# Linear attention in a hybrid decoder trunk: the products of two levels, and those between token tiles, sent in one burst

## The chip, the cores and the metric

The kernel runs on one core of a Trainium2 chip, as one launch. The metric is the device time of one execution in microseconds, the median of several runs. Engines are named as in the profile: TensorE is PE (its weight loads PEld), VectorE DVE, ScalarE ACT, GpSimd POOL, SyncE SP.

## The reference

Two layers (DEPTH), 512 tokens, a width of 2048. Each layer normalises its input, multiplies it by one input projection, feeds three groups of heads from the result (a short convolution, a stick-breaking attention, a gated linear attention), gates each of them, and puts the concatenation through an output projection into the residual stream. The change lies in the gated linear attention, which has four heads with 64 key and 128 value columns:

```python
g = jax.nn.log_sigmoid((gl_lr @ gla_w_up + gla_b_up)) / GLA_TAU
def step(state, inp):                       # one chunk of 64 tokens
    qc, kc, vc, gc = inp
    cum = jnp.cumsum(gc, axis=2)
    o_inter = jnp.einsum("bhck,bhkv->bhcv", qc * jnp.exp(cum), state)
    diff = cum[:, :, :, None, :] - cum[:, :, None, :, :]
    decay = jnp.where(causal, jnp.exp(jnp.minimum(diff, 0.0)), 0.0)
    att = jnp.einsum("bhtk,bhsk,bhtsk->bhts", qc, kc, decay)
    o_intra = jnp.einsum("bhts,bhsv->bhtv", att, vc)
    ...
    return new_state, o_inter + o_intra
```

In words: each token attends to itself and all earlier ones, with a weight that is a product of query, key and a decay of its own for every key column. The output is normalised and gated before it joins the mix.

## The kernel before

**Projections.** The weights are in float32 and are streamed from memory, 256 columns at a time. ACT makes the high half of each block in float16 (`whi`, line 476, or `split` in `wsums`, line 530) and DVE the low half (`wlo`, line 483, or line 531). TensorE multiplies high by high, high by low and low by high, with the activations held as two halves too. These products use the whole array of 128 rows: lines 729 to 731 (`project_cols`), 740 to 742 (`tok_mm`), and line 822 or 825 (`prod` in `project_quick`, which uses seven products of half blocks where there were eight).

**The linear attention without a scan.** The weights of all pairs of tokens within a token tile of 128 are built by halving. At the level with half length `h` (64, 32, 16, 8, 4, 2, 1, in `LEV`) each block of 2h tokens splits into a source half and a target half; the decay between the two halves is the product of one factor of the source and one of the target, so that an ordinary product of matrices gives all weights of that level. DVE and ACT make both factors (the tile `e`; lines 1130 to 1139). Then each is split into two float16 pieces: the source by `split_src` (high on ACT, line 1095, low on DVE, line 1096; tile `qp` in the profile), the target by `split_tgt` (high on ACT, line 1101, low on DVE, line 1102; tile `th`). There are two slots for pieces, `src16[b]` and `tgt16[b]`, and the levels use them in turn, `b = li % 2`.

`mm3` (line 1104) does the products: three terms, each for the two heads of a pair. A head has 64 key columns, so each product of line 1109 uses 64 rows of the array and the two heads lie in different halves of it. A level needs four calls (one for each token tile) of six products, into a PSUM tile `aps` (`psz` in the profile, two buffers of two banks). A masked copy on DVE (line 1144) puts the level into `attd` (tile `zw`), which collects all levels. The diagonal (lines 1153 to 1163) follows; its products are on line 1158.

**Between token tiles** the weights factor with a single reference point, in two sets (`two` = 0 and 1, lines 1167 to 1179), with the same slots and the same `mm3`: four calls, lines 1186 to 1190. Their sums are read on ACT (line 1193) and DVE (line 1194); then line 1206 multiplies everything by the values.

All of this is done for two head pairs, `p` = 0 and 1, in each of the two layers. Work of other parts goes on at the same time.

**The order of the work.** Behind a short hand-ordered start a planner sets the order of each engine's queue, from an estimate of times and from priorities: work written earlier goes first if it is ready, and a block under `tc.high_priority` goes ahead of that. Every engine then takes its queue strictly in that order and waits where a semaphore isn't there yet. `order(a, b)` makes the planner place `a` behind `b`. In the kernel before, the products of `mm3` have no priority and no order of their own: the planner puts them in where they are ready, between products of the projection that is running at the time.

Of the kernel before, what the change touches and what calls it, by code (L numbers as in the profile page):

```python
# [11 lines left out]
ALU = mybir.AluOpType  # L12
# [5 lines left out]
P = 128  # L18
# [25 lines left out]
def hybrid_trunk(ctx, tc, x, norm_g, w_in, conv_w, conv_b, sb_qn_g, sb_kn_g,  # L44
                 gla_w_up, gla_b_up, gla_on_g, w_out, out):
    nc = tc.nc
    V, S, G, T = nc.vector, nc.scalar, nc.gpsimd, nc.tensor
# [3 lines left out]
    NT = seq // P  # L51
# [19 lines left out]
    def nm(s):  # L71
        uid[0] += 1
        return f"{s}_{uid[0]}"
# [4 lines left out]
    def wk(shape, tag, bufs=None, dt=F32):  # L78
        return work.tile(shape, dt, tag=tag, name=nm(tag), bufs=bufs)
# [7 lines left out]
    def bank2():  # L87
        return psz.tile([P, 2, 512], F32, tag="z", name=nm("psz"))
# [59 lines left out]
    HT = P // 2  # L148
# [132 lines left out]
    for h in range(2):  # L281
        mm = spread(h)
# [430 lines left out]
    for l in range(depth):  # L713
# [287 lines left out]
        for t, o, u in project_by_token(xh, xl, GX):  # L1001
# [16 lines left out]
        for p in range(2):  # L1018
# [3 lines left out]
            a = wk([P, seq], "ga")  # L1022
# [19 lines left out]
        src16 = [[scr[0][:, b, i, :] for i in range(2)] for b in range(2)]  # L1042
        tgt16 = [[scr[1][:, b, i, :seq // 2] for i in range(2)] for b in range(2)]
# [5 lines left out]
        for tag in ("qT", "kT"):  # L1049
            o = wk([P, 2, seq], tag)  # L1050
# [47 lines left out]
        def split_tgt(e, b):  # L1098

            hi, lo = tgt16[b]  # L1100
            S.activation(hi, e, AF.Copy)
            V.tensor_tensor(lo, e, hi, ALU.subtract)

        def mm3(o, sb, ss, tb, g0, g1):

            for i, (a, b) in enumerate(((0, 0), (0, 1), (1, 0))):
                for hh in range(2):
                    hs = slice(hh * HT, (hh + 1) * HT)
                    T.matmul(o[:, hh, :], src16[sb][a][hs, ss], tgt16[tb][b][hs, g0 * HT:g1 * HT], start=i == 0,
                             stop=i == 2, skip_group_check=True)  # L1110

        tsl = [slice(t * P, (t + 1) * P) for t in range(NT)]
        for p in range(2):
            Pp, q_, k_ = Pc[:, p, :], gq[:, p, :], gk[:, p, :]
            attd = wk([P, 2, NT, P], "zw")
            G.memset(attd, 0.0)

            for li, h in enumerate(LEV[:-1]):
                b = li % 2
                e = wk([P, 2, seq // 2], "e")  # L1120

                def sides(a):
                    a4 = a.rearrange("p (b s j) -> p b s j", s=2, j=h)
                    return a4[:, :, 0, :], a4[:, :, 1, :]

                (P0, P1), (k0, _), (_, q1) = sides(Pp), sides(k_), sides(q_)
                e0, e1 = (e[:, i, :].rearrange("p (b j) -> p b j", j=h) for i in range(2))
                if h > 1:
                    ref = P0[:, :, h - 1:h].to_broadcast([P, seq // (2 * h), h])
                    V.tensor_tensor(e0, P0, ref, ALU.subtract)  # L1130
                    V.tensor_tensor(e1, ref, P1, ALU.subtract)
                    S.activation(e, e, AF.Exp, scale=1.0 / TAU)
                    V.scalar_tensor_tensor(e0, e0, 1.0, k0, ALU.min, ALU.mult)
                    split_src(e0, lambda a: sides(a)[0], b)
                else:
                    V.tensor_tensor(e1, P0, P1, ALU.subtract)
                    S.activation(e[:, 1, :], e[:, 1, :], AF.Exp, scale=1.0 / TAU)
                    split_src(k_, lambda a: a, b)
                V.scalar_tensor_tensor(e1, e1, 1.0, q1, ALU.min, ALU.mult)
                split_tgt(e[:, 1, :], b)  # L1140
                aps = bank2()[:, :, :NT * HT]
                for t in range(NT):
                    mm3(aps[:, :, t * HT:(t + 1) * HT], b, tsl[t], b, t, t + 1)
                V.copy_predicated(
                    attd.rearrange("p h t (b s j) -> p h (t b) s j", s=2, j=h)[:, :, :, 1, :],
                    masks[:, li].rearrange("p (o t) (b j) -> p o (t b) j", o=1, j=h).to_broadcast(
                        [P, 2, NT * HT // h, h]),
                    aps.rearrange("p h (t b j) -> p h (t b) j", t=NT, j=h))

            e = wk([P, seq], "e")  # L1150
            V.tensor_tensor(e, q_, k_, ALU.mult)
            hi, lo = src16[1]
            S.activation(hi, e, AF.Copy, scale=2.0 ** -14)
            V.scalar_tensor_tensor(lo, e, 2.0 ** -14, hi, ALU.mult, ALU.subtract)
            aps = bank2()[:, 0, :2 * NT]
            for t in range(NT):
                for i, a in enumerate((hi, lo)):
                    T.matmul(aps[:, 2 * t:2 * t + 2], a[:, tsl[t]], heads, start=t == i == 0, stop=i == 1,
                             skip_group_check=True)
# [7 lines left out]
            for two, bias in ((0, (nT[:, p, 0:1], None, nT[:, p, 2:3], None)),  # L1167
                              (1, (nT01[:, p:p + 1], nT[:, p, 1:2], None, nT[:, p, 2:3]))):
                e = wk([P, 2, 256], "e")
                n = [0, 0]  # L1170
                for t in range(NT):
                    tgt = int(t >= 2 if two else t % 2)
                    et = e[:, tgt, n[tgt] * P:(n[tgt] + 1) * P]
                    n[tgt] += 1
                    S.activation(et, Pp[:, tsl[t]], AF.Exp, scale=(-1.0 if tgt else 1.0) / TAU,
                                 bias=bias[t] if bias[t] is not None else 0.0)
                    V.scalar_tensor_tensor(et, et, 1.0, (q_ if tgt else k_)[:, tsl[t]], ALU.min, ALU.mult)
                split_src(e[:, 0, :], lambda a: a[:, :256], two)
                split_tgt(e[:, 1, :], two)

            for i in range(NT):
                S.activation(att16[0][:, i], attd[:, :, i], AF.Copy, scale=2.0 ** -21)
                V.scalar_tensor_tensor(att16[1][:, i], attd[:, :, i], 2.0 ** -21, att16[0][:, i], ALU.mult, ALU.subtract)
            ax = [wk([P, 2, 512], tag, dt=F16) for tag in ("za", "za", "e")]
            aps = bank2()
            mm3(aps[:, :, :128], 0, tsl[0], 0, 0, 2)
            mm3(aps[:, :, 128:256], 0, tsl[1], 0, 2, 4)
            mm3(aps[:, :, 256:], 1, tsl[0], 1, 0, 4)
            aps2 = bank2()
            mm3(aps2[:, :, :256], 1, tsl[1], 1, 0, 4)  # L1190
            for a, o in zip(ax, (aps[:, :, :256], aps[:, :, 256:], aps2[:, :, :256])):
                hi, lo = (a[:, i].rearrange("p (h c) -> p h c", h=2) for i in range(2))
                S.activation(hi, o, AF.Copy, scale=2.0 ** -21)
# [2 lines left out]
            for hh in range(2):  # L1196
# [7 lines left out]
                for i, (cs, t, a) in enumerate(seqmm):  # L1204
                    for n, (vi, ai) in enumerate(((0, 0), (0, 1), (1, 0))):
                        T.matmul(ops_[:, cs], gv[p][:, vi, t, hh * P:(hh + 1) * P], a[ai], start=i == n == 0,
                                 stop=i == len(seqmm) - 1 and n == 2, skip_group_check=True)
# [181 lines left out]
        for j in range(4):  # L1389
# [21 lines left out]
            for n in range(2):  # L1411
# [11 lines left out]
                for b in range(2):  # L1423
# [149 lines left out]
```

## Time and profile before

| | us |
|---|---|
| median of 3 runs | 1629.07 (1628.01 to 1629.4) |
| the profiled execution | 1628.53 |
| its span, first to last instruction | 1626.7 |
| TensorE busy | 1614.1 (99%) |
| weight loads | 1355.0 (83%) |
| VectorE busy | 1446.8 (89%) |
| ScalarE busy | 1196.5 (74%) |
| GpSimd busy | 274.0 (17%) |

Busy times are of the profiled execution. A row of the timeline gives start and duration in us, the engine, the line, what is written and read, the shape, and how many instructions were merged in it; a bracket at its end tells how long the engine stood idle before it and what ended that. A TensorE instruction's duration spans its way through the array, and the next starts before it ends, so that distances between starts tell what a product costs. A table by stretch gives for each engine the busy time in it. The linear attention of layer 0 lies between 125 and 280 us of the span, that of layer 1 between 930 and 1090.

### The profile page before, as it was taken

Reading aid. Unit: us, or ns where it says so; the run is one execution under the profiler, and the core shown is the slowest. Engines: PE = TensorE matmul, PEld = TensorE weight load, DVE = VectorE, ACT = ScalarE, POOL = GpSimd, SP = SyncE. Lnnn points to the kernel's source line nnn. Section 1 sums busy time; section 2 is a strip of 40 time slices with the busy share of each in tenths; the row PEclk is TensorE's granted clock in tenths of the full one; section 3 lists DMA queues with packets and bytes.
Section 4 is the critical chain, followed back from the end, with each engine's and each line's share of the span. In section 5 each row is a group of like instructions: output and inputs, shape, how many; then the busy total and the mean of one; then the engine's idle time right before and its main releaser. Section 6 shows DMA issues by size and latency. Waiting matters only on the chain.

```text
span 1626.7 us, 42256 instructions
## 1 busy us (share of the span) xinstructions
PE 1614.1 (99%) x18205; PEld 1355.0 (83%) x18205; DVE 1446.8 (89%) x2411; ACT 1196.5 (74%) x1769; POOL 274.0 (17%) x305
## 2 busy tenths in 40 slices
PE   8999999999999999999999999999999999999998
PEld 6757768989898967799996668689898989668998
DVE  8989999989898979898699899898988889898896
ACT  8579887868787776666775788788787868676573
POOL 0122121121212122011102111211121211220110
PEclk9999999999999999999999999999999999999999
DMA  7335245476867677544734444545777786773441
GB/s 264 106 78 168 67 125 132 122 143 154 149 148 164 150 169 216 157 156 144 238 89 114 121 118 118 138 84 142 152 159 157 154 166 154 167 226 127 156 157 54
DMA packets 193643, 235.98 MB, mean 145 GB/s; under 512 B 90242, under 2 KB 153036, under 8 KB 192944
## 3 DMA queue, kind: packets, MB, share of 16 engines
q0 software_dynamic: 79904, 181.42, 42.1%
q1 hardware_dynamic: 104544, 42.42, 13.0%
q10 hardware_dynamic: 9008, 9.45, 1.7%
q8 instruction: 142, 2.33, 0.6%
q14 instruction: 45, 0.37, 0.1%
HBM read 179.65 MB, written 14.68 MB: 119 GB/s over the span
## 4 chain that ended last, share of the span: by engine, by line
PE 79%; DVE 11%; ACT 6%; issue 2%; DMA 1%; POOL 0%; SPq 0%; DVEq 0%; ACTq 0%; POOLq 0%
PE psp L825 25%; PE psp L822 15%; PE psp L884 6%; PE psp L742 6%; PE psp L741 6%; PE psp L740 6%; PE psp L730 4%; PE psp L729 4%; PE psp L731 3%; DVE wl L531 2%; PE psm L1379 2%; PE psz L1339 1%; ACT wh L530 1%; ACT junk L404 1%; DMA x<-in_x_dram 1%
## 5 line engine op out<-in xcount | busy, mean ns | idle before, releaser
L530 ACT ACTIVATE wh<-st,ws 128x1024 f16<-128x1024 f32 x270 | 300.6, 1144 | 172.3 <-DVE st L550 93.7
L531 DVE SCALAR_TENSOR_TENSOR wl<-st,ws,wh 128x1024 f16<-128x1024 f32 x270 | 339.9, 1281 | 29.1 <-ACT wh L530 29.0
L404 ACT ACTIVATE junk<-st 128x2048 uint8<-128x2048 f32 x150 | 285.4, 1903 | 14.2 <-DMA st<-in_w_in_dram 7.3
L822 PE MATMUL psp<-s,wh 128*128 128x256 f16 x1280 | 217.8, 273 | 0.5 <-DVE g L838 0.4
L822 PEld LDWEIGHTS <-wh 128*128 128x128 f16 x1920 | 187.5, 98 | 23.6 <-issue 1.8
L825 PE MATMUL psp<-wh,s 128*128 128x128 f16 x2048 | 177.0, 219 | 0.0
L822 PE MATMUL psp<-s,wl 128*128 128x256 f16 x640 | 174.4, 273 | 0.9 <-DVE wq L433 0.5
L740 PE MATMUL psp<-wh,m 128*128 128x256 f16 x640 | 174.5, 273 | 0.0
L742 PE MATMUL psp<-wh,m 128*128 128x256 f16 x640 | 174.5, 273 | 0.0
L741 PE MATMUL psp<-wl,m 128*128 128x256 f16 x640 | 174.5, 273 | 0.0
L825 PEld LDWEIGHTS <-s 128*128 128x128 f16 x3072 | 173.0, 98 | 0.7 <-issue 0.6
L825 PE MATMUL psp<-wl,s 128*128 128x128 f16 x1024 | 173.3, 219 | 0.0
L483 DVE SCALAR_TENSOR_TENSOR wl<-st,ws,wh 128x2048 f16<-128x2048 f32 x62 | 145.0, 2348 | 13.2 <-ACT wh L476 12.5
L383 POOL DMA_DIRECT2D st<-in_w_in_dram x114 | 110.4, 1043 | 243.8 <-DVE w7l L531 114.3
L825 PEld LDWEIGHTS <-m 128*128 128x128 f16 x2448 | 139.2, 98 | 2.2 <-issue 1.6
L420 POOL PARTITION_ALL_REDUCE wgm<-wm x75 | 52.8, 704 | 454.4 <-ACT junk L404 426.5
L476 ACT ACTIVATE wh<-st,ws 128x2048 f16<-128x2048 f32 x60 | 118.6, 1999 | 14.0 <-DVE ws L437 5.5
L407 POOL DMA_DIRECT2D st<-st x36 | 57.2, 1588 | 367.4 <-ACT junk L404 357.0
L822 PEld LDWEIGHTS <-wl 128*128 128x128 f16 x960 | 93.9, 98 | 14.6 <-issue 2.2
L825 PE MATMUL psp<-wh,m 128*128 128x128 f16 x1088 | 97.2, 219 | 0.4 <-DVE ws L437 0.4
L825 PE MATMUL psp<-wl,m 128*128 128x128 f16 x544 | 93.0, 219 | 0.0
L731 PEld LDWEIGHTS <-wl 128*128 128x128 f16 x384 | 37.6, 98 | 44.0
(451 smaller groups left out, 4187.2 us busy)
## 6 DMA issues: line engine op xcount, KB each, us to landing
st<-in_w_in_dram POOLq DMA_DIRECT2D x114, 1024.0 KB, 8.4
st<-in_w_out_dram POOLq DMA_DIRECT2D x32, 1024.0 KB, 8.2
st<-st POOLq DMA_DIRECT2D x36, 512.0 KB, 6.9
st<-in_w_in_dram SPq DMA_DIRECT2D x6, 1024.0 KB, 11.7
mixd<-g POOLq DMA_DIRECT2D x20, 256.0 KB, 7.0
x<-in_x_dram SPq DMA_DIRECT2D x4, 1024.0 KB, 5.2
qT<-in_x_dram ACTq DMA_DIRECT2D x8, 512.0 KB, 4.1
qT<-xs ACTq DMA_DIRECT2D x8, 512.0 KB, 12.3
```

Source lines behind the costliest of these rows:

```text
L383: load = queue.dma_start(s_, src[l, h * HK * P:(h + 1) * HK * P, c0:c0 + GW].rearrange("(k p) n -> p k n", p=P), max_dma_last_dim=1024)
L404: sq = S.activation(junk(HK * GW).rearrange("p (k n) -> p k n", k=part.shape[1]), part, AF.Square, accum_out=peak[i][:, h:h + 1])
L476: hi = S.activation(wh[:, :, :GW], staged[i][h], AF.Copy, scale=scales[i])
L483: a = V.scalar_tensor_tensor(wl[:, :, :GW], staged[i][h], scales[i], wh[:, :, :GW], ALU.mult, ALU.subtract)
L530: hi = S.activation(h_, b, AF.Copy, scale=sc)
L531: V.scalar_tensor_tensor(l_, b, sc, h_, ALU.mult, ALU.subtract)
L740: T.matmul(o, ah[:, t, k, :], wh[:, kk, :n], start=st_, stop=False, skip_group_check=True)
L741: T.matmul(o, ah[:, t, k, :], wl[:, kk, :n], start=False, stop=False, skip_group_check=True)
L742: return T.matmul(o, al[:, t, k, :], wh[:, kk, :n], start=False, stop=en, skip_group_check=True)
L822: mm = T.matmul(o, w[q_][:, kk, :], a[p_][:, :, kk, :], start=st_, stop=en, skip_group_check=True)
L825: mm = T.matmul(o[:, t * P:(t + 1) * P], a[p_][:, t, kk, :], w[q_][:, kk, :], start=st_, stop=en, skip_group_check=True)
L884: mm = T.matmul(o[:, :n], a_[:, t, k, :], w[k // HK][part][:, k % HK, :n], start=i == 0 and k == 0, stop=i == 2 and k == KT - 1)
```

## The change

`split_tgt` returns its last instruction, the low piece on DVE. `mm3` takes its three terms in another order (high by high last), and with a new argument `behind` it places its products behind an instruction; it returns its last product.

In the first head pair a level with `b` = 0 and `h` > 1 stops once its pieces are made. The level after it then sends the products of both: its own and, into the other half of the same PSUM tile, those of the level before; then two masked copies follow, first that of the earlier level. So seven levels make three pairs and a single one (h = 1). In the second head pair each level sends its own products. All are placed behind the last piece, each group of six behind the group before it, at a priority above all other work. The products between token tiles are ordered in the same way, behind the last piece of the second set, beginning with the second set.

```diff
-            V.tensor_tensor(lo, e, hi, ALU.subtract)
+            return V.tensor_tensor(lo, e, hi, ALU.subtract)

-        def mm3(o, sb, ss, tb, g0, g1):
+        def mm3(o, sb, ss, tb, g0, g1, behind=None):
-            for i, (a, b) in enumerate(((0, 0), (0, 1), (1, 0))):
+            for i, (a, b) in enumerate(((0, 1), (1, 0), (0, 0))):
                 for hh in range(2):
                     hs = slice(hh * HT, (hh + 1) * HT)
-                    T.matmul(o[:, hh, :], src16[sb][a][hs, ss], tgt16[tb][b][hs, g0 * HT:g1 * HT], start=i == 0,
-                             stop=i == 2, skip_group_check=True)
+                    mm = T.matmul(o[:, hh, :], src16[sb][a][hs, ss], tgt16[tb][b][hs, g0 * HT:g1 * HT], start=i == 0,
+                                  stop=i == 2, skip_group_check=True)
+                    if behind is not None:
+                        order(mm, behind)
+            return mm
...
-                split_tgt(e[:, 1, :], b)
-                aps = bank2()[:, :, :NT * HT]
-                for t in range(NT):
-                    mm3(aps[:, :, t * HT:(t + 1) * HT], b, tsl[t], b, t, t + 1)
-                V.copy_predicated(
-                    attd.rearrange("p h t (b s j) -> p h (t b) s j", s=2, j=h)[:, :, :, 1, :],
-                    ...
+                ready = split_tgt(e[:, 1, :], b)
+                if not b and h > 1 and not p:
+                    continue
+                aps, mm = bank2(), ready
+                pair = (li, li - 1) if b and not p else (li,)
+                for n, lj in enumerate(pair):
+                    for t in range(NT):
+                        o = n * NT * HT + t * HT
+                        with tc.high_priority(offset=1 << 20):
+                            mm = mm3(aps[:, :, o:o + HT], lj % 2, tsl[t], lj % 2, t, t + 1, mm)
+                for n, lj in reversed(list(enumerate(pair))):
+                    j = LEV[lj]
+                    V.copy_predicated(
+                        attd.rearrange("p h t (b s j) -> p h (t b) s j", s=2, j=j)[:, :, :, 1, :],
+                        ...
+                        aps[:, :, n * NT * HT:(n + 1) * NT * HT].rearrange("p h (t b j) -> p h (t b) j", t=NT, j=j))
...
-                split_tgt(e[:, 1, :], two)
+                ready = split_tgt(e[:, 1, :], two)
...
             aps = bank2()
-            mm3(aps[:, :, :128], 0, tsl[0], 0, 0, 2)
-            mm3(aps[:, :, 128:256], 0, tsl[1], 0, 2, 4)
-            mm3(aps[:, :, 256:], 1, tsl[0], 1, 0, 4)
             aps2 = bank2()
-            mm3(aps2[:, :, :256], 1, tsl[1], 1, 0, 4)
+            with tc.high_priority(offset=1 << 20):
+                mm = mm3(aps[:, :, 256:], 1, tsl[0], 1, 0, 4, ready)
+                mm = mm3(aps2[:, :, :256], 1, tsl[1], 1, 0, 4, mm)
+                mm = mm3(aps[:, :, :128], 0, tsl[0], 0, 0, 2, mm)
+                mm3(aps[:, :, 128:256], 0, tsl[1], 0, 2, 4, mm)
```

More of the change, by code (lines that the diff above doesn't have):

```diff
@@ L1139, in hybrid_trunk @@
                 V.scalar_tensor_tensor(e1, e1, 1.0, q1, ALU.min, ALU.mult)
-                split_tgt(e[:, 1, :], b)
-                aps = bank2()[:, :, :NT * HT]
-                for t in range(NT):
-                    mm3(aps[:, :, t * HT:(t + 1) * HT], b, tsl[t], b, t, t + 1)
-                V.copy_predicated(
-                    attd.rearrange("p h t (b s j) -> p h (t b) s j", s=2, j=h)[:, :, :, 1, :],
-                    masks[:, li].rearrange("p (o t) (b j) -> p o (t b) j", o=1, j=h).to_broadcast(
-                        [P, 2, NT * HT // h, h]),
-                    aps.rearrange("p h (t b j) -> p h (t b) j", t=NT, j=h))
+                ready = split_tgt(e[:, 1, :], b)
[12 more added lines that the diff above has]
+                        attd.rearrange("p h t (b s j) -> p h (t b) s j", s=2, j=j)[:, :, :, 1, :],
+                        masks[:, lj].rearrange("p (o t) (b j) -> p o (t b) j", o=1, j=j).to_broadcast(
+                            [P, 2, NT * HT // j, j]),
+                        aps[:, :, n * NT * HT:(n + 1) * NT * HT].rearrange("p h (t b j) -> p h (t b) j", t=NT, j=j))
             e = wk([P, seq], "e")
```

## The prediction

> **What bounds the kernel now.** I read the page first (busy shares, clock, chain of waits), then the busy times by stretch around the linear attention, then the timeline of TensorE there, then the timelines of VectorE (DVE) and ScalarE (ACT) at the places where TensorE stands still.
>
> ```profile
> span 1626.7 us, 42256 instructions
> PE 1614.1 (99%) x18205; PEld 1355.0 (83%) x18205; DVE 1446.8 (89%) x2411; ACT 1196.5 (74%) x1769; POOL 274.0 (17%) x305
> PEclk9999999999999999999999999999999999999999
> PE 79%; DVE 11%; ACT 6%; issue 2%; DMA 1%; POOL 0%; SPq 0%; DVEq 0%; ACTq 0%; POOLq 0%
> ```
>
> TensorE is busy for 99% of the span at a full clock in every slice, and 79% of the chain that ends last lies on it. The next engine is DVE with 89%. So an interval taken from TensorE shortens the run, as long as DVE isn't what TensorE would otherwise wait for. That has to be asked of the stretches that the change touches: first head pair and second head pair of layer 0 (first and third row), what lies between them, and the same three of layer 1.
>
> ```profile
> core 0: us, PE busy (x) PEld busy (x) DVE busy (x) ACT busy (x) POOL busy (x), PEclk, DMA share, GB/s
> 125.00:190.00 65.00, 64.49 (x652) 45.57 (x651) 62.88 (x130) 57.58 (x95) 12.32 (x11) 1.00 0.43 110
> 190.00:226.00 36.00, 36.00 (x289) 27.92 (x287) 34.56 (x61) 30.89 (x43) 7.24 (x8) 1.00 0.55 181
> 226.00:280.00 54.00, 54.00 (x595) 39.97 (x594) 51.47 (x97) 39.19 (x66) 9.32 (x10) 1.00 0.39 79
> 930.00:990.00 60.00, 59.56 (x604) 41.77 (x602) 58.34 (x121) 54.60 (x91) 8.87 (x10) 1.00 0.42 103
> 990.00:1040.00 50.00, 50.00 (x364) 34.77 (x363) 42.89 (x65) 40.03 (x52) 8.23 (x11) 1.00 0.41 133
> 1040.00:1090.00 50.00, 50.00 (x627) 42.44 (x626) 50.00 (x100) 36.16 (x65) 9.07 (x10) 1.00 0.53 121
> sum 315.00, PE 314.05 PEld 232.44 DVE 300.14 ACT 258.45 POOL 55.05; mean PE 52.34 PEld 38.74 DVE 50.02 ACT 43.08 POOL 9.17
> ```
>
> Here DVE is nearly as full as TensorE: 300.14 of 315 us against 314.05. TensorE is short of time by 0.95 us only, and DVE has 14.86 us idle, most of it (7.11 us) between the two head pairs of layer 1 and none at all in 1040 to 1090. Both engines bound these stretches together; this is the difficulty of the forecast.
>
> **The price of an interruption.** The 64-row products of line 1109 are thrown between the 128-row products of a projection. In the timeline of TensorE (start, duration, engine, line):
>
> ```profile
> 132.86 0.64 PE L1109 MATMUL psz<-th,qp 64*128 64x64 f16 x31
> 149.78 0.27 PE L822 MATMUL psp<-x,w7l 128*128 128x256 f16 x1
> 149.89 0.27 PE L822 MATMUL psp<-x,w7h 128*128 128x256 f16 x1
> 150.10 0.84 PE L1109 MATMUL psz<-th,qp 64*128 64x64 f16 x46
> 150.87 0.39 PE L729 MATMUL psp<-x,wh 128*128 128x512 f16 x1
> 157.79 0.38 PE L729 MATMUL psp<-x,wh 128*128 128x512 f16 x1
> 158.10 0.20 PE L1109 MATMUL psz<-th,qp 64*128 64x64 f16 x2
> 158.24 0.39 PE L730 MATMUL psp<-x,wh 128*128 128x512 f16 x1
> 158.46 0.38 PE L731 MATMUL psp<-x,wl 128*128 128x512 f16 x1
> 159.67 0.81 PE L1109 MATMUL psz<-th,qp 64*128 64x64 f16 x44
> 160.41 0.39 PE L729 MATMUL psp<-x,wh 128*128 128x512 f16 x1
> 177.28 0.61 PE L1109 MATMUL psz<-th,qp 64*128 64x256 f16 x8
> 177.82 0.28 PE L822 MATMUL psp<-x,wl 128*128 128x256 f16 x1
> 1079.95 1.00 PE L1109 MATMUL psz<-th,qp 64*128 64x128 f16 x20
> ```
>
> A 128x256 product starts 0.11 us after the one before it (149.78 to 149.89), a 128x512 one 0.22 us (158.24 to 158.46). From 157.79 to 158.24 pass 0.45 us, so a run of two small products adds 0.23 us. From 149.89 to 150.87 pass 0.98 us, so a run of 46 adds 0.87 us. The difference, 0.64 us for 44 products, is 0.0145 us each; two of them are worth 0.03, and 0.20 us is what a run costs whatever its length. The whole trace has 53 such runs, the first at 132.86 and the last at 1079.95: 14 and 14 in the head pairs of layer 0, 12 and 13 in those of layer 1. That is 10.6 us for going in and out.
>
> **The change part by part.**
>
> *Fewer runs.* In the first head pair seven levels become three bursts of 48 and one of 24, and the products between token tiles become one burst of 24: 5 runs. In the second, seven bursts of 24 and one: 8 runs. Together 26 for two layers. Saved on TensorE: (14-5), (14-8), (12-5), (13-8), that is 9, 6, 7 and 5 runs, times 0.20: 1.8, 1.2, 1.4 and 1.0 us, 5.4 us in all. The number of products, their weight loads and their widths stay, and the other order of the three terms costs nothing.
>
> *What of it reaches the end.* At the end of the first head pair TensorE stands still in both layers, for low parts of weights that DVE splits behind its share of the linear attention:
>
> ```profile
> 184.40 0.28 PE L822 MATMUL psp<-s,wl 128*128 128x256 f16 x1 [0.51 <-DVE wq L433]
> 985.51 0.28 PE L822 MATMUL psp<-s,wl 128*128 128x256 f16 x1 [0.44 <-DVE wl L531]
> 183.07 1.27 DVE L531 SCALAR_TENSOR_TENSOR wl<-st,ws,wh 128x1024 f16<-128x1024 f32 x1
> 984.17 1.28 DVE L531 SCALAR_TENSOR_TENSOR wl<-st,ws,wh 128x1024 f16<-128x1024 f32 x1
> ```
>
> The split that ends at 184.34 releases the product at 184.40, the one that ends at 985.45 that at 985.51. If TensorE came there earlier and DVE did not, it would wait the more: these splits are what is late next. The saving of the first pairs (1.8 + 1.4 = 3.2 us) passes only as far as DVE comes earlier. DVE idles 65.00 - 62.88 = 2.12 and 60.00 - 58.34 = 1.66 us in these two stretches, and part of that hangs on results of TensorE. The bounds are 0 and 3.2; I take half, 1.6, between them. For the second pairs (1.2 + 1.0 = 2.2) no such standstill is in the rows, and DVE has 36.00 - 34.56 = 1.44 us idle before that of layer 0, 54.00 - 51.47 = 2.53 in it, and 7.11 before that of layer 1; I take all 2.2, with 0 as the other end. Sum: 3.8 us.
>
> *Waiting for the last piece.* No product of a level now starts before the level's low target piece (line 1102) is split. The copy at line 1144 needs all products of its level, so the two that used to go ahead (158.10, the rest at 159.67) had made nothing earlier: 0. Of a pair the first level's copy comes a level later; the sums `attd` are not read before all levels are in, so this costs 0, with no bound but the order on DVE. POOL and SP issue nothing new and are not moved past anything.
>
> *The products between token tiles* are held until both sets of pieces are there. ACT reads their sums here:
>
> ```profile
> 181.72 0.58 ACT L1193 ACTIVATE za<-psz 128x512 f16<-128x512 f32 x1
> 161.07 0.61 ACT L1095 ACTIVATE qp<-kT 128x512 f16<-128x512 f32 x1
> 156.66 0.42 DVE L1102 TENSOR_TENSOR th<-e,th 128x256 f16<-128x256 f32 x1
> ```
>
> TensorE is done with them at 177.82 and ACT comes at 181.72, 3.9 us later; in that cover the delay costs 0, and without it at most the way from the first to the last of the old runs.
>
> *The slots.* Pieces have two slots, used in turn. A first level used to give its slot back before the second was begun; now both are held until the burst, and ACT's split of the next level (line 1095) queues behind that, with the weight splits behind it on ACT and DVE. In the rows DVE's last piece ends at 157.08 and its products run from 159.67 to 160.41: TensorE is 2.6 us behind DVE, and ACT refills a slot at 161.07, 0.7 us after they end. The lower end is 0 (ACT has other work to do until then). The upper end is 2.6 us and a burst of 48, 0.9 us (by the run of 46), for one boundary; after such a wait TensorE is no longer behind, so once in a layer: 7.0 us. I take 0, the row at 161.07 being the nearest: it shows a refill that comes without being late.
>
> The profiled execution took 1628.53 us around its span of 1626.7; the median is 1629.07. From the median, 1629.07 - 3.8 = 1625.3. About 0.2%, 3.3 us, is what a measurement of this kernel can tell from no change.
>
> **The rivals.**
>
> *A, my forecast:* most of the saving gets through, 1625.3; with all 5.4 and both standstills (0.95) gone 1622.7.
>
> *B, DVE is the limit:* the first pairs give nothing and the second pairs half, 1.1 us: 1628.0. For it speak 58.34 of 60 and 50.00 of 50 us of DVE and the two standstills; against it DVE's 14.86 idle us, and that the planner draws DVE's order anew. The Trainium skill, Perfetto Trace Analysis, section Identifying the Most-Contended Engine, says that TensorE's matmul occupancy does not tell its headroom and that the share of weight loading does. By that rule DVE (89%) stands ahead of TensorE (83%) and the gain is B's; the two standstills agree with it, the 79% of the chain do not.
>
> *C, slower, by the slots:* the refill waits behind the burst, 3.5 us in each layer: 1625.3 + 7.0 = 1632.3. It decides when the refill is queued less than 3.5 us after the pair's last piece and DVE has no other ready work. The 0.7 us at 161.07 speak for it; ACT's idle 7.42 us in 125 to 190 against it.
>
> *D, the bursts do not hold:* each group of six products is tied to the last of the group before it; if the planner puts projection products into each seam, a head pair has 7x4+4 = 32 runs, 128 in all, 75 more than 53: 15 us, 1644. The new priority speaks against it, and so does the run of 46.
>
> **How the numbers follow.** A 0.45, B 0.31, C 0.19, D 0.05. A is the likeliest, with its own range 1622.7 to 1625.8. Faster by over 0.2% is A, 0.45; within it B, 0.31; slower C and D, 0.24. The range leaves out D and the edge of C, and reaches 1.7 us under A's lower end for an order of DVE that removes waits which I cannot price: 1621.0 to 1632.5.
>
> **What the changed profile would show.** Right: 26 runs of line 1109, none of two products, bursts of 48 adding about 0.9 us, and no longer standstills at the end of the first pairs. Half right: as many runs, but TensorE waits there by 1 us or more for line 531. Wrong: idle time of ACT before line 1095 released by TensorE, or runs of six. What would make it wrong without any of that is a new order of DVE's splits elsewhere that lets TensorE wait.

## The result, and the profile after

The changed kernel takes 1639.01 us (median of 6 runs, 1638.32 to 1640.03) against 1628.63 for the kernel before (1627.82 to 1629.4): a ratio of 1.0064, 95% interval 1.0053 to 1.0075. It is 10.4 us slower; 1625.3 was forecast, with 1632.5 as the upper end.

The lines of the page after, which answer to those of before:

```profile
span 1637.4 us, 42231 instructions
PE 1611.3 (98%) x18205; PEld 1355.8 (83%) x18205; DVE 1448.6 (88%) x2411; ACT 1197.9 (73%) x1769; POOL 273.6 (17%) x305
PE 75%; DVE 13%; ACT 7%; issue 2%; DMA 2%; POOL 0%; SPq 0%; DVEq 0%; ACTq 0%; POOLq 0%
```

TensorE's own work has fallen (1614.1 to 1611.3 us), the span has grown by 10.7, and 4 points of the chain have gone from TensorE to DVE, ACT and DMA. The busy times by stretch tell where. The columns are those of the table in the prediction; the last two rows lie around one standstill.

```profile
125.00:190.00 65.00, 63.42 (x648) 45.98 (x647) 62.83 (x129) 57.79 (x95) 12.19 (x11) 1.00 0.43 108
190.00:226.00 36.00, 33.68 (x279) 26.44 (x277) 27.46 (x41) 25.61 (x29) 5.23 (x7) 1.00 0.55 182
226.00:280.00 54.00, 48.62 (x515) 35.29 (x514) 51.21 (x100) 39.35 (x70) 10.77 (x9) 1.00 0.37 74
280.00:330.00 50.00, 48.63 (x713) 44.99 (x712) 44.16 (x74) 39.67 (x67) 8.36 (x10) 0.97 0.38 102
930.00:990.00 60.00, 59.32 (x602) 42.18 (x600) 57.77 (x126) 54.72 (x89) 10.49 (x12) 1.00 0.48 123
1040.00:1090.00 50.00, 49.50 (x569) 39.15 (x567) 50.00 (x103) 37.28 (x68) 10.23 (x11) 1.00 0.43 88
1090.00:1130.00 40.00, 37.64 (x597) 35.70 (x595) 36.14 (x55) 33.56 (x52) 5.28 (x6) 1.00 0.44 118
275.00:279.60 4.60, 0.78 (x8) 0.45 (x5) 4.60 (x11) 2.57 (x6) 0.00 (x0) 1.00 0.00 2
279.80:283.30 3.50, 3.44 (x19) 2.53 (x20) 3.50 (x8) 1.34 (x4) 0.30 (x1) 0.58 0.02 5
```

The stretches of before that the prediction does not show:

```profile
280.00:330.00 50.00, 49.73 (x773) 47.36 (x771) 44.50 (x69) 41.84 (x71) 7.99 (x9) 1.00 0.60 151
1090.00:1130.00 40.00, 39.53 (x668) 37.92 (x666) 37.05 (x62) 34.52 (x60) 8.30 (x9) 1.00 0.49 133
```

TensorE is now short of 1.58, 2.32, 5.38 and 1.37 us in the first four rows (layer 0), and of 0.68, 0.50 and 2.36 in the next three; before, it was short of 0.51, 0, 0 and 0.27 in the first four and of 0.44, 0 and 0.47 in the others. DVE worked 34.56 of 36 us between the two head pairs of layer 0 before; now it works 27.46. Those 7.1 us of work come later, when the second pair needs DVE too. What TensorE waited for longest, beside 3.1 us at line 257, which it waited before too (engine, tile and line, who released it; total, times, longest):

```profile
PE psp L822 <- DVE wl L531: 7.0, 4, 4.1
PE psp L825 <- DVE raw L851: 3.1, 2, 1.7
PE psp L822 <- ACT qT L843: 1.9, 1, 1.9
```

TensorE's timeline, one burst and the longest standstill:

```profile
144.94 0.27 PE L822 MATMUL psp<-s,wh 128*128 128x256 f16 x1
145.15 0.87 PE L1109 MATMUL psz<-th,qp 64*128 64x64 f16 x48
145.95 0.28 PE L822 MATMUL psp<-s,wh 128*128 128x256 f16 x1
...
275.40 0.38 PE L822 MATMUL psp<-s,wh 128*128 128x256 f16 x2
279.86 0.28 PE L822 MATMUL psp<-s,wl 128*128 128x256 f16 x1 [4.07 <-DVE wl L531]
...
280.68 0.42 PE L822 MATMUL psp<-s,wl 128*128 128x256 f16 x1
280.89 0.63 PE L822 MATMUL psp<-s,wh 128*128 128x256 f16 x2
```

A burst of 48 adds 145.95 - 144.94 - 0.11 = 0.90 us, as priced. The products that start at 279.86 wait for a low part that DVE begins at 278.52. From 275.24 to 278.52 DVE has other work ahead of it: pieces and factors of the second pair (lines 1096, 1102 and 1188) and, for somewhat more than half of the time, other operations (lines 555, 423 and 1411). ACT and DVE show where the second pair was held up:

```profile
215.83 1.91 ACT L404 ACTIVATE junk<-st 128x2048 uint8<-128x2048 f32 x1 [3.84 <-DMA st<-in_w_in_dram]
218.68 1.91 ACT L404 ACTIVATE junk<-st 128x2048 uint8<-128x2048 f32 x1 [0.84 <-DMA st<-in_w_in_dram]
220.59 0.67 ACT L1224 ACTIVATE e<-psz,gu 128x512 f32<-128x512 f32 x1
```

```profile
200.88 0.16 DVE L423 TENSOR_TENSOR wq<-wgm 128x1 f32<-128x1 f32 x1 [4.08 <-POOL wgm L420]
278.52 1.28 DVE L531 SCALAR_TENSOR_TENSOR wl<-st,ws,wh 128x1024 f16<-128x1024 f32 x1
```

The second normalisation of the first pair (line 1224 now, 1212 before) begins at 220.59; before:

```profile
204.50 0.67 ACT L1212 ACTIVATE e<-psz,gu 128x512 f32<-128x512 f32 x1
```

It now begins 16 us later. In ACT's queue the squares of weights (line 404) stand ahead of it and wait for transfers. Up to 200.88 DVE's queue stands for 4.08 us behind a scale that hangs on such squares. The second pair's first burst runs at 241.16; in the kernel before its first products ran at 228.18.

### The profile page after: what moved, and what is told of

The parts are those of the page before. It is cut to its first block, busy times and chain, and to the rows that moved or that the text cites. A ratio compares the mean times of both kernels' runs of the same rounds, so it can differ in the third digit from the quotient of the medians.

```text
span 1637.4 us, 42231 instructions
## 1 busy us (share of the span) xinstructions
PE 1611.3 (98%) x18205; PEld 1355.8 (83%) x18205; DVE 1448.6 (88%) x2411; ACT 1197.9 (73%) x1769; POOL 273.6 (17%) x305
## 4 chain that ended last, share of the span: by engine, by line
PE 75%; DVE 13%; ACT 7%; issue 2%; DMA 2%; POOL 0%; SPq 0%; DVEq 0%; ACTq 0%; POOLq 0%
PE psp L825 25%; PE psp L822 13%; PE psp L884 6%; PE psp L740 5%; PE psp L741 5%; PE psp L742 5%; PE psp L729 4%; PE psp L730 4%; PE psp L731 4%; DVE wl L531 3%; PE psm L1391 2%; ACT wh L530 1%; PE psz L1351 1%; ACT junk L404 1%; DVE zw L1155 1%
```

## The experiments

In all but the free ones (e4, e8, l15, c16) the order of DVE's and ACT's queues is given, by a chain of order edges over each engine's instructions. In t9, g12, v17 and v18 TensorE's queue is given too; in the others the planner draws TensorE's queue anew, and their times hold that as well. "Small copies" means that the masked copies take only a small part of each level, so that most of each level's sums are left out of the result; these runs serve only to take load off DVE. Each ratio is to the kernel before in the same measurement.

```diff
+    for eng, seq_ in PINNED:
+        made = [i for i in nc.cur_bb.bb.instructions if i.engine == eng]
+        for a, b in zip(seq_, seq_[1:]):
+            tc.add_manual_dep(made[b], made[a].name, <no semaphore, order only>)
```

| run | us | kernel before | ratio, 95% interval |
|---|---|---|---|
| p1, bursts, order of before | 1631.88 | 1628.94 | 1.0019, 1.0010 to 1.0028 |
| p2, no bursts, order of after | 1655.67 | 1628.94 | 1.0165, 1.0151 to 1.0179 |
| p3, single levels, order of before | 1631.49 | 1628.94 | 1.0018, 1.0009 to 1.0026 |
| e4, single levels, free | 1634.13 | 1628.94 | 1.0032, 1.0020 to 1.0044 |
| t5, before, small copies | 1634.81 | 1629.01 | 1.0035, 1.0021 to 1.0049 |
| t6, bursts, small copies | 1623.45 | 1629.01 | 0.9966, 0.9954 to 0.9979 |
| t9, t5 with TensorE's order of before | 1626.31 | 1628.70 | 0.9985, 0.9976 to 0.9994 |
| e7, one wait moved | 1640.34 | 1629.01 | 1.0069, 1.0057 to 1.0082 |
| e8, normalisation with priority | 1639.99 | 1629.01 | 1.0067, 1.0054 to 1.0079 |
| w10, old order 186 to 241 us | 1632.09 | 1628.70 | 1.0026, 1.0017 to 1.0035 |
| w11, old order 186 to 335 us | 1631.48 | 1628.70 | 1.0016, 1.0007 to 1.0025 |
| n13, only the normalisations | 1648.44 | 1628.63 | 1.0125, 1.0109 to 1.0140 |
| r14, all but them | 1646.80 | 1628.63 | 1.0112, 1.0098 to 1.0126 |
| l15, bursts of levels alone, free | 1634.52 | 1628.63 | 1.0037, 1.0024 to 1.0050 |
| c16, burst between tiles alone, free | 1633.72 | 1628.63 | 1.0034, 1.0021 to 1.0047 |
| g12, low pieces on GpSimd | 1715.90 | 1628.70 | 1.0536, 1.0522 to 1.0551 |
| v17, p1 with four moves | 1627.88 | 1628.52 | 0.9993, 0.9984 to 1.0002 |
| v18, p1 with seven moves | 1628.11 | 1628.42 | 0.9996, 0.9987 to 1.0005 |

### The order or the products: p1, p2, p3, e4

p1 and p2 change the given order alone; p3 and e4 change this in the kernel after:

```diff
-                if not b and h > 1 and not p:
-                    continue
-                pair = (li, li - 1) if b and not p else (li,)
+                pair = (li,)
```

> The kernel after with all its products as they are (levels of the first pair two to a burst), but VectorE and ScalarE issue their work in the order of the kernel before; only the copy of the earlier level of a pair comes later, right ahead of the copy of the later one. Theory 1 (the bursts save what they were priced at, 5.4 us on TensorE, and the loss comes from the new order that the planner draws for VectorE and ScalarE): between 1623 and 1629 us, 10 us or more under the 1639.0 of the kernel after, and the standstill of 4.1 us at the low parts of line 531 near 276 us is gone. Theory 2 (the products themselves cost it: two levels held together, copies that come late, slots that come free late, the priority of the products): 1637 to 1641, with or without that order.

> The kernel before with all its products as they were (no bursts held together, no priority), but VectorE and ScalarE issue their work in the order of the kernel after. Theory 1 (the order): as slow as the kernel after or slower by what the bursts save, 1637 to 1646 us, with a standstill of 3 us or more at line 531 near 276 us. Theory 2 (the products): 1627 to 1631.

> Bursts in both head pairs, but one level to a burst everywhere (no level waits for another), the products between token tiles in one burst, and VectorE and ScalarE in exactly the order of the kernel before. 32 runs of line 1109 instead of 53, so 21 x 0.20 = 4.2 us less on TensorE. Theory 1: 1624 to 1628.5 us, faster than before by as much of the 4.2 as VectorE lets through (if VectorE is the limit: 1627 to 1628.5). Theory 2, priority and waiting cost it: 1632 or more.

> The same products as in the run with single levels (32 runs of line 1109), but the planner draws the order of VectorE and ScalarE itself. Theory 1: the time is that of whatever order comes out; it differs from the run with the order of before by 2 us or more, and the difference stands in TensorE's waits for low parts (lines 531, 851) in 190 to 330 us. Theory 2, pairs are what costs: the same as that run within 2 us, and under 1631.

p1 is 2.9 us over before where the kernel after is 10.4 over, with the same products: 7.5 us hang on the order of the queues, and the standstill of 4.1 us is gone. (TensorE's queue is not quite that of the kernel after, since the planner drew it again.) It missed the expected 1629 by 3 us and is slower than before. p2 went further than expected, +26.7 us, and not by the standstill that was expected: its longest wait for line 531 is 0.7 us. So an order is fitted to its products, and the wrong pair costs more than either part. That is a warning for p1 too: its 2.9 us over before need not all be the bursts'. p3 missed as well: 1631.49 lies between 1628.5, up to which theory 1 had it, and 1632, from which theory 2 had it. It equals p1 within the scatter, so holding two levels together costs nothing that shows against one. e4 is 2.6 us slower than p3 with the same products, as theory 1 had it, though of the waits that it named in 190 to 330 us only the one for line 851 is there (1.4 us), beside 1.8 us for line 838. Theory 2 is out as the cause of the 10.4 us. Whether the products cost the 2.9 and 2.5 us of p1 and p3, these four runs do not tell. In p1 the stretches read:

```profile
125.00:190.00 65.00, 62.67 (x643) 45.66 (x642) 63.10 (x130) 58.01 (x95) 11.76 (x11) 1.00 0.43 109
280.00:330.00 50.00, 47.96 (x752) 45.54 (x751) 44.39 (x69) 40.88 (x69) 8.09 (x10) 1.00 0.59 152
1040.00:1090.00 50.00, 47.80 (x604) 41.26 (x602) 50.00 (x101) 36.35 (x66) 10.74 (x11) 1.00 0.52 122
```

TensorE's own work in p1 is 1607.7 us, 6.4 less than before, so the bursts do save about what they were priced at. The saving has become idle time: TensorE is busy for 62.67 of 65 us where it was for 64.49, and for 47.80 of 50 where it was for 50.00, while DVE is at 63.10 (62.88 before) and at 50.00 of 50 in both.

### Is it VectorE: t5, t6, t9

```diff
                 V.copy_predicated(
-                    attd.rearrange("p h t (b s j) -> p h (t b) s j", s=2, j=h)[:, :, :, 1, :],
+                    attd.rearrange("p h t (b s j) -> p h (t b) s j", s=2, j=h)[:, :1, :1, 1, :],
```

The masks and the sums read are shortened alike; in t6 the same is done at line 1155.

> The kernel before, VectorE and ScalarE in its own order, but each of the 28 copies of a level (line 1144, 0.73 us each) takes only the first columns of one head and one token tile, so most of each level's sums are left out of the result. VectorE has some 0.5 us less for each, 3.5 us in each head pair; products, waits and order stay. Theory 1 (VectorE is the limit in the head pairs of the bursts): TensorE was short of only 1.7 us between 125 and 330 and 930 and 1170 us, so this kernel, without bursts, gains little: 1625 to 1628.5. Theory 2 (the bursts fail for a reason of their own): the same.

> The kernel of the run with the bursts and the old order (levels of the first pair two to a burst, VectorE and ScalarE in the order of before), with the same small copies, so the same part of the result left out. Theory 1: with VectorE relieved by some 14 us the 5.8 us that TensorE saves come through: 3 to 6 us faster than the kernel before with small copies, 1620 to 1624. Theory 2 (late bursts, late copies or late slots delay the work whatever VectorE's load is): no faster than the kernel before with small copies, by 1 us at most, or slower as it was with full copies (1631.9 against 1628.9).

> The kernel before with the same small copies as the earlier run (the same part of the sums left out), and now TensorE, too, issues in exactly the order of the kernel before, so that only the copies' length differs from it. In the earlier run the planner had redrawn TensorE's order and put a level's products ahead of pieces that were not there: standstills of 4.9 us at 150 to 155 us. Theory 1 (VectorE is the limit only once TensorE gets ahead; before is bound by both): 1626 to 1628.5, and the kernel with bursts and small copies (1623.45) is 3 to 5 us faster than this one. Theory 2 (the short copies alone brought that time): 1622 to 1625, no slower than with bursts.

t5 came out as neither theory had it (1625 to 1628.5), and told something by it: the planner, seeing shorter copies, drew TensorE's queue anew, and TensorE met pieces that were not there:

```profile
150.32 0.58 PE L1109 MATMUL psz<-th,qp 64*128 64x64 f16 x27
151.39 0.21 PE L1109 MATMUL psz<-th,qp 64*128 64x64 f16 x2 [0.49 <-ACT th L1101]
152.36 0.50 PE L1109 MATMUL psz<-th,qp 64*128 64x64 f16 x22 [0.77 <-DVE th L1102]
154.32 0.61 PE L729 MATMUL psp<-x,wh 128*128 128x512 f16 x1 [1.47 <-ACT wh L476]
156.71 0.61 PE L731 MATMUL psp<-x,wl 128*128 128x512 f16 x1 [1.35 <-DVE wl L483]
```

t9 has the same instructions with TensorE's order of before. It is 2.4 us under before where t5 is 5.8 over: 8.2 us by the order of TensorE's queue alone. t9 is then the measure for t6, the one without bursts, the other with, though t6's TensorE queue is still one that the planner drew. With small copies the bursts gain: 0.9966 / 0.9985 = 0.9981, 3.1 us (about 0.6 to 5.5 from the two intervals), the lower edge of what theory 1 expected. With full copies and the same order of DVE and ACT (p1) they lost 2.9, so relieving DVE is worth about 6 us to the bursts. The stretches of t9, then of t6:

```profile
125.00:190.00 65.00, 65.00 (x660) 46.29 (x659) 60.51 (x131) 57.26 (x95) 11.79 (x11) 1.00 0.45 118
1040.00:1090.00 50.00, 50.00 (x639) 42.59 (x637) 47.78 (x100) 37.27 (x64) 9.43 (x10) 1.00 0.50 117
```

```profile
125.00:190.00 65.00, 64.38 (x670) 47.42 (x668) 60.45 (x131) 57.76 (x96) 11.64 (x11) 1.00 0.46 118
1040.00:1090.00 50.00, 50.00 (x656) 43.65 (x654) 48.37 (x103) 39.31 (x67) 9.59 (x10) 1.00 0.53 119
```

DVE is now 1.6 to 4.6 us under full. In 1040 to 1090 TensorE is full in both, and its saving shows as more instructions done in the same stretch (656 against 639). So DVE's load is one of the things that keep the saving back: with room on DVE the bursts gained here, with full copies they had not.

### Where in the order: e7, e8, w10, w11, n13, r14

e7, w10, w11, n13 and r14 are the kernel after with its own order of DVE and ACT given in the same way, and with parts of these lists changed. e8:

```diff
-            while not p and norms:
-                norms.pop(0)()
+            with tc.high_priority(offset=1 << 20):
+                while not p and norms:
+                    norms.pop(0)()
```

> The kernel after with its own order of VectorE and ScalarE, with one group moved in each queue: on ScalarE the two squares of line 404 at 195 and 198 us, two splits of line 530 and the copy of line 850 go behind the first normalisation's Exp and Square (lines 1229, 1230); on VectorE the four small operations of the scale that hangs on those squares (lines 423, 433, 437, 439) go behind the convolution's line 862. Theory 1 (the place where the new order loses is VectorE's wait of 4.08 us before line 423 at 200.88): that wait is gone, the standstill of 4.1 us before line 822 near 276 shrinks below 1.5, and the time is 1631 to 1636. Theory 2 (the loss is not from that wait but from the second pair as a whole coming late): within 1.5 us of 1639.

> The kernel after, with the normalisations that follow the first head pair (lines 1224 to 1236) given the same high priority as the products; the planner draws the order anew. Theory 1 (the two normalisations come late, hold both e buffers and push the second pair's levels into the projection whose low parts VectorE has to split): the second pair begins before 232 us as in the kernel before, and the time is 1628 to 1634. Theory 2 (the place of the second pair doesn't matter): within 2 us of 1639.

> The kernel after, with VectorE's and ScalarE's work that it starts between 186 and 241 us (normalisations of the first pair, weight squares and splits ahead of the second pair's levels) put back into the order that it has in the kernel before; all else as in the kernel after. Theory 1a (the loss is sown here: the second pair begins late): the standstill of 4.1 us near 276 us shrinks below 1.5 us and the time is 1630 to 1634. Theory 1b (it is made later, by the order in which the second pair's work and the low parts of the projection are mixed): 1637 or more.

> The same for all that the kernel after starts between 186 and 335 us on VectorE and ScalarE, the second pair of layer 0 included. Both forms of theory 1: 1630 to 1634, as with the old order in the whole kernel (1631.9). If it stays above 1636 the loss is not from the order in this stretch, and what the old order won in the whole kernel was won elsewhere.

> The kernel after; in the stretch of 186 to 241 us only the first pair's two normalisations and the pieces made from them (lines 1224 to 1236, 954, 955) go back to where they stand among the other work in the kernel before; the squares, scales and splits of the weights keep the order of the kernel after. Theory 1n (the late normalisations are the cause: they hold both e buffers, and the second pair begins late): 1630 to 1634, standstill near 276 us below 1.5 us. Theory 1r (the weights' squares and splits are): 1636 to 1640.

> The counterpart: in the same stretch all but those operations (splits, squares, scales, the convolution, the first levels) goes into the old order, and the normalisations stay at the place among them that they have in the kernel after. Theory 1n: 1636 to 1640. Theory 1r: 1630 to 1634.

e7 took the wait of 4.08 us away and won nothing, as its second theory had it. DVE now waits there for ACT's splits, and the standstill at 276 us stays at 4.1:

```profile
200.16 1.28 DVE L531 SCALAR_TENSOR_TENSOR wl<-st,ws,wh 128x1024 f16<-128x1024 f32 x1 [3.56 <-ACT wh L530]
```

e8 tells nothing: the priority moved no normalisation earlier (the second begins at 221.00). w10 is the answer as to the place: 55 us of two queues put back leave 3.4 us of the 10.4. TensorE's 27 runs of line 1109 are there of the same sizes and in the same order as in the kernel after (p1 has 25), so these 7.0 us are due to DVE's and ACT's order. There the second normalisation begins at 205.88 and the second pair's first burst runs at 230.65, and of TensorE's waits for the low parts this is left (total, times, longest):

```profile
PE psp L822 <- DVE wl L531: 4.0, 3, 2.5
```

The longest, 2.5, is above the 1.5 expected; the time is within what was expected. w11 wins 0.6 more, no more than the medians scatter. n13 and r14 were to split the cause and didn't: each half of the old order with the other half of the new one is worse than the whole new order, by 9.4 and 7.8 us (19.8 and 18.2 over before). In n13 the second normalisation comes early (210.18), and yet the second pair's first burst runs at 247.54, later than in the kernel after. TensorE has these waits, the second of which isn't there in the kernel after:

```profile
PE psp L822 <- DVE wl L531: 6.0, 4, 4.1
PE psp L729 <- ACT wh L476: 4.0, 1, 4.0
```

So neither half brings any of the loss back by itself; and since each mixture makes standstills of its own, neither run shows what a half would cost alone. What is shown is that the sequence of 186 to 241 us as a whole makes 7.0 of the 10.4 us; which of its pairs matter stays open.

### Which part makes the planner redraw: l15, c16

l15 is the kernel after with this taken back; c16 is the kernel before with this and the new `mm3` alone:

```diff
+            with tc.high_priority(offset=1 << 20):
+                mm = mm3(aps[:, :, 256:], 1, tsl[0], 1, 0, 4, ready)
+                mm = mm3(aps2[:, :, :256], 1, tsl[1], 1, 0, 4, mm)
+                mm = mm3(aps[:, :, :128], 0, tsl[0], 0, 0, 2, mm)
+                mm3(aps[:, :, 128:256], 0, tsl[1], 0, 2, 4, mm)
```

> The kernel after with the bursts of levels, but the products between token tiles as in the kernel before (in four pieces, each as soon as its operands are there, no priority). The planner draws the order anew. If the bursts of levels make it draw the slower order: 1636 to 1642. If the burst between token tiles does: 1628 to 1633.

> The kernel before with the products between token tiles in one burst and the levels as they were. If the burst between token tiles makes the planner draw the slower order: 1636 or more. If not, TensorE saves some 8 runs less or 1.6 us and VectorE keeps it: 1627 to 1631.

Both came out between what either answer expected, 5.9 and 5.1 us over before. With e4, e8 and the kernel after these are five programs with the planner free, and all are 5 us or more over before. No part of the change is the culprit by itself. That the redrawn order makes the loss is shown for the kernel after (7.5 us by p1) and for e4 (2.6 us by p3); for l15 and c16 it is likely, but they were not timed with the order of before.

### Can the saving pass with all work in place: g12, v17, v18

g12, in `split_tgt`; v17 and v18 change the lists of the given order alone:

```diff
-            return V.tensor_tensor(lo, e, hi, ALU.subtract)
+            return G.tensor_tensor(lo, e, hi, ALU.subtract)
```

> The kernel with the bursts and the old order, but the 36 low target pieces of line 1102 (0.42 us each on VectorE) are made by GpSimd; VectorE and ScalarE otherwise as in that run, TensorE in that run's order too. 15 us less on VectorE. Theory 1 (VectorE's load holds back what the bursts save): 1622 to 1627, faster than that run (1631.9) and than before (1628.9), if GpSimd is as quick. Against it: GpSimd also issues the loads of the weights and the sums over partitions, and a load behind a waiting piece comes late; then TensorE waits for products of line 1109 or for low parts, 1633 or more.

> The run with the bursts and the old order (1631.9, TensorE's order as there), with four single moves, each at a standstill of TensorE in its trace: line 555 behind the next split of line 531 at 182 and at 984 us (2.3 and 1.5 us), line 838 ahead of the products' factors of line 1188 at 1075 us (2.2 us), and on ScalarE the copy of line 843 ahead of the second split of line 476 at 324 us (1.3 us). Theory 1 in its mild form (the order is not fitted to the bursts, some of the saving can pass): 1626 to 1630. In its strict form (VectorE's load alone decides; what is moved ahead delays what is behind it): 1631 or more.

> The run with four moves (1627.9), and three more at the standstills left in its trace: line 851 ahead of one split of line 531 at 312 and at 1113 us (0.6 and 1.3 us), and on ScalarE a split of line 530 ahead of line 1268 at 180 us (1.3 us). If the saving passes as far as the order is fitted: 1625.5 to 1627.5, under before by 1 to 3 us. If VectorE's load decides: 1627.5 or more, each wait only moves on.

g12 relieves DVE and loses 87 us, so it doesn't answer the question: 50.4 us of TensorE's time go into waiting for GpSimd's pieces.

```profile
PE psz L1109 <- POOL th L1102: 50.4, 8, 11.7
```

v17 is 0.6 us under before where p1 was 2.9 over: four moves win 3.6 us, so p1's loss was a bad fit of order and products, and not the products' own. It comes to 1627.88, and before to 1628.52 on the same chip: the interval of the ratio holds 1. TensorE's own work is 1608.8 us, 5.3 less than before, and 4.5 us of that have become idle time. Three more moves (v18) bring nothing; the wait for line 851 near 1113 us is gone and this one has come up, at 1119:

```profile
PE psp L825 <- DVE ws L437: 1.6, 1, 1.6
```

DVE in v18 is at 63.10 of 65 us in the first stretch and 50.00 of 50 in 1040 to 1090, as in before (62.88 and 50.00). By the bounds expected for it v17 is the mild form of theory 1 (1626 to 1630; the strict form had 1631 or more), and v18 says that DVE's load decides (1627.5 or more). Together: fitting the order wins back what p1 lost, and then the gain stops within the scatter of the kernel before. None of these versions with all work in place beats it beyond that; v17's interval leaves room for up to 2.6 us, and whether a better order would let more pass stays open.

## Why the prediction failed, point by point

*Fewer runs: right in size.* There are 27 runs of line 1109 instead of the 26 forecast, and not the same ones: in each first pair the first burst came split into 2 and 46 products and the last into 2 and 22, while in the second pairs three times two bursts came as one. 26 fewer at 0.20 is 5.2 us against 5.4, and TensorE's own work fell by 6.4 in p1 and 5.3 in v17. Bursts of 48 add 0.90 us. That the first level of a pair waits for the second costs nothing agrees with p3 and p1 being equal; the other order of the terms and the wait for the last piece were not timed by themselves.

*What of it reaches the end: this step failed, twice.* First, 3.8 of 5.4 us were to pass: half for the first pairs, and all 2.2 for the second pairs, because DVE had 1.44 and 7.11 us idle before them and 2.53 in the one of layer 0. That was too much room: the 7.11 us lie where no burst is, and in the second pair of layer 1 itself DVE is full (50.00 of 50 in 1040 to 1090). With the order fitted, 0.6 and 0.3 us pass (v17, v18), which can't be told from 0; with DVE relieved it was 3.1 (t6 against t9). Rival B, DVE is the limit, had 1628.0, and v17 and v18 are at 1627.9 and 1628.1. The rule weighed in the prediction from the Trainium skill, Perfetto Trace Analysis, section Identifying the Most-Contended Engine (judge TensorE by its weight loads, not by its matmul time), gave B; these runs agree with it, DVE being at 89%, ahead of the 83% of weight loads though behind the 99% of TensorE's busy time.

*Second, and the larger part:* "with no bound but the order on DVE" and "B ... against it ... that the planner draws DVE's order anew" put the redrawing down as free, or as a help. It is a cost: 10.4 - 2.9 = 7.5 us by p1, and 10.4 + 0.6 = 11.0 by v17, against an order fitted by hand. The prediction named this in its last sentence on what would make it wrong, a new order of DVE's splits elsewhere that lets TensorE wait, and gave it no price and no chance. The rows before had a sign of it: DVE's 34.56 of 36 us between the pairs leave 1.44 us for any wait at the head of its queue, and the split that TensorE needs next is behind it. They gave no figure for the loss.

*The sign of half right* came: TensorE waits for line 531 at the end of the first pair of layer 0, in two standstills of 1.0 and 0.6 us (63.42 of 65 us busy against 64.49). *The slots (C)* cost nothing that shows in the first pairs; ACT's line 1095 waited for the products once, in the second pair of layer 1, 2.0 us. *The seams (D)* opened four times, at the runs of two products, and not between all groups of six.

## What to carry to other kernels

Where two engines are both nearly full, expect time taken from one to pass only in those stretches where the other has room; sum the idle time of the other engine there, not over the whole region. Where a planner orders the queues, every edit is also a new draw of the order: give that draw a range of its own, on the side of a loss too, above all where the tightest queue has little slack. To learn what the edit itself is worth, time it with the order of before given, refitted at the few standstills that this brings, and with the second engine relieved; give the order of every queue that the planner could redraw. Halves of two orders mixed can be worse than either, as n13 and r14 were.

## What the runs showed of the hardware that was not expected

After the standstill of 4.07 us in the kernel after TensorE ran slower. From 280.68 to 280.89 pass 0.21 us between 128x256 products that otherwise start 0.11 apart, and the granted clock in 279.80 to 283.30 is 0.58: some 1.5 us more (14 products by 0.10). The Trainium skill, TensorE: Matmul & The Clock Gate, Part 1, says that the clock falls to half after an idle window of about 3.4 us. The standstill here agrees. Shorter ones went with it too. In c16 there were two, with a single product between them:

```profile
274.61 0.22 PE L825 MATMUL psp<-wh,x 128*128 128x128 f16 x1 [0.67 <-ACT wh L530]
276.43 0.27 PE L822 MATMUL psp<-x,wh 128*128 128x256 f16 x1 [1.60 <-DVE g L838]
277.02:280.43 3.41, 3.41 (x19) 2.43 (x17) 3.41 (x9) 0.53 (x2) 1.26 (x2) 0.50 0.65 198
```

The granted clock (third figure from the right) is 0.50 for 3.41 us. In t5 the standstills shown above, each of 0.49 to 1.47 us, went with 0.50 from 153.61 to 160.44. A single one of 2.46 us in w10, before 274.24, brought nothing: the granted clock is 1.00 behind it. So in this kernel the length of one standstill doesn't tell whether the clock falls, and some standstills of under 2 us cost more than their length. It also differs between executions of one kernel: of p1's eleven, the three with a granted clock of 1.000 took 1630.6 us, the six with 0.998 or less 1631.6 to 1634.1. So a part of p1's 2.9 us may be this; the execution that its profile shows is one of the three.

GpSimd pays for changing between kinds of work. In g12:

```profile
167.88 0.41 POOL L420 PARTITION_ALL_REDUCE wgm<-wm  x1 [6.25 <-issue]
175.10 1.03 POOL L1102 TENSOR_TENSOR th<-e,th 128x256 f16<-128x256 f32 x1 [6.81 <-issue]
```

The piece itself takes 1.03 us; 6.81 us before it, and 6.25 before the sum over partitions, the engine waited for nothing that the profile shows. There are nine such waits before line 1102 (53.6 us) and nine before line 420 (58.7 us); in p1, where no pieces are made there, line 420 has none. The Trainium skill, GPSIMD Engine Reference, section 2.1 Instruction dispatch, gives about 6 us for loading code at the first call to a freshly loaded kernel; these rows agree.
